# Two experts in four column groups of 32, attention scores over full 128 rows, a subtraction moved to VectorE

## Chip, cores and metric

The kernel runs on one core of a Trainium2 chip, as one launch. The metric is the device time in microseconds (us). Before the change the median of three runs was 2307.31 us (2302.57 to 2308.02). The profile shows one further execution of the same program.

## What is computed

256 tokens of width 1024 in fp32 go through two blocks. The first has a convolution, a forgetting attention and a mixture of 32 experts (four per token); of it the change touches only one place in the code. The second block, cut to what matters:

```python
def second_block(x, ...):
    x = layer_norm_2(x, ln_emb_g, ln_emb_b)
    for layer in range(2):
        mix = hybrid_mixer(x, w_in[layer], ..., decay_fwd[layer], decay_bwd[layer], ...)
        x = layer_norm_2(DEEPNORM_ALPHA * x + mix, ln1_g[layer], ln1_b[layer])
        ffn = swiglu(x, ...) if layer == 0 else moe_swiglu(x, ...)
        x = layer_norm_2(DEEPNORM_ALPHA * x + ffn, ln2_g[layer], ln2_b[layer])

def moe_swiglu(x, router_w, router_b, w1, w3, w2):      # 8 experts, width 1408, two per token
    logits = x @ router_w + router_b
    top_vals, top_idx = lax.top_k(logits, 2)
    gate = ...                                          # softmax of the two, 0 elsewhere
    for e in range(8):
        out = out + gate[..., e:e + 1] * ((silu(x @ w1[e]) * (x @ w3[e])) @ w2[e])
```

The mixer holds a windowed attention (8 query heads, 2 key heads of width 64: scores = q kᵀ / 8) and a retention whose decays are log_sigmoid(decay_fwd) and log_sigmoid(decay_bwd). With the reference's own inputs the router gives the 8 experts of the second block 57, 123, 49, 9, 8, 49, 165 and 52 tokens.

## The kernel before

**Products.** Where full precision is wanted, each fp32 operand is split into a high part that TensorE takes in one pass (type fp32r) and a low rest. A product is then three matmuls, high·high, high·low, low·high (`mm3`, L305 to L307); the weights are split on the fly by a cast on ACT (L325) and a subtraction on DVE (L328). Where few rows stand against many weights, the weights are used unsplit as fp32 moving data (types f32 on both sides), which appear in the trace as two records for each matmul.

**Weights.** `load` (L243) brings tiles of 128 x 2048 fp32 (1 MB) on SP's DMA queue into a ring; in the second mixture the ring has 8 tiles. A tile's load waits on SP until the ring's tile is released, and the loads stand in a fixed order on the queue.

**Order of the work.** The program is written against a Tile layer whose scheduler fixes the order of the instructions on each engine by costs of its own; the code's order is its input. So an edit in one place can reorder work that it doesn't name.

**Stages** (us from the start of the span): preparation, conditioning and the first block's mixer 0 to 250, the first mixture 250 to 1221, mixer 0 of the second block to 1440, its dense part to 1633, mixer 1 to 1837, second mixture's router and expert 0 to 1929, experts 1, 2 and 3 to 2095, experts 4, 5 and 6 to 2252, expert 7 to 2289, the last norm to the end.

**Mixer.** For each pair of heads j the scores are 8 matmuls (L1358 and L1359, taken in turn): `qa[:, j, i]` holds 64 rows of the query's high part and 64 of its low part, `kk[:, i]` the key's high part on both halves, so L1358 takes two of the three products over 128 rows. L1359 takes the third, the query's high part with the key's low part, over 64 rows. `kk` is filled at L1308 (ACT) and L1310 (DVE). There are 8 pairs in the two mixers. The decays' log_sigmoid (L287 to L302, tile `lsg`) stands at the start of the second block, into `lgam`.

**Second mixture.** Experts are sorted by their number of tokens, and `ROOM2` gives the room of each position p: expert 1, the largest, takes all 256 rows (`expert_all`), 0, 4, 5, 6 have room for 128 (`expert_128`), 2, 3 and 7, the smallest, room for 64 (`expert_64`). A token that finds no room goes to an extra loop at the end (L1817), which takes a chunk of up to 128 rows through `expert_128`; the loop's count is read on the chip. Rows are gathered by one-hot matmuls (`gather2`, L1589 to L1605) from `xtp`, the split of the normed input, whose low part is a GpSimd subtraction (L1569).

`expert_64` has weights of two hidden tiles f in hand (each 128 wide, gate and up beside each other: 256 columns). For each of 8 k it issues one matmul per f, with the 64 gathered rows as stationary operand and 256 columns of weights moving (L1732); f even goes to columns 0 to 63 of the array, f odd to 64 to 127. `finish` takes silu on ACT, multiplies on DVE, transposes on PE (L1718), copies on ACT. For the second product (L1748), 512 columns move, the halves of the output in the two column groups. FT2 is 11, so the sixth f-pair has one f. Expert 1's steps alternate with those of 2 and 3: one step of expert 1 (48 mm3 matmuls), then two steps of the others (one f-pair, since an f-pair is two steps).

Of the kernel before, what the change touches and what calls it, by code (L numbers as in the profile page):

```python
# [19 lines left out]
P = 128  # L20
# [19 lines left out]
ROOM2 = [128, 256, 64, 64, 128, 128, 128, 64]  # L40
# [175 lines left out]
def two_blocks(ctx: ExitStack, tc: tile.TileContext, I, out, dbg=None, upto=None):  # L216
# [47 lines left out]
    xres = keep.tile([P, 2, D], F32, name="xres")  # L264
    nc.sync.dma_start(cols, I["cols"])
# [613 lines left out]
    with ExitStack() as pb:  # L879
# [217 lines left out]
        for p in range(NE1):  # L1097
            while (p, CHK1[p][-1]) not in ready or group[2] and p in [g[0] for g in group[1]]:
                gather_on(8)
            if p == 0:  # L1100
                w1, w2 = first_w1, (lambda kk: first_w[8 + kk])
            elif p < FIX1:
                w1 = lambda k: second_w[k] if k < PRE1 else load(I["wei"][p, k * P:(k + 1) * P, :])
                w2 = lambda kk: load(I["weo"][p, kk * 256:(kk + 1) * 256, :].rearrange("(k p) d -> p k d", p=P))
            else:
                er = nc.sync.value_load(route.oi[0:1, p:p + 1], min_val=0, max_val=NE1 - 1)
                w1 = lambda k: load(I["wei"][bass.ds(er, 1), k * P:(k + 1) * P, :].rearrange("a p c -> p (a c)"))
                w2 = lambda kk: load(I["weo"][bass.ds(er, 1), kk * 256:(kk + 1) * 256, :].rearrange("a (k p) d -> p (a k) d", p=P))
            expert1(w1, w2, [ready[p, c] for c in CHK1[p]], lambda: places(p), b1p[:, p] if p else b10, gather_on)
            if p == 8:  # L1110
                second_biases()
                route.extra()
                n_extra = nc.values_load(route.tot[0:1, 0:1], min_val=0, max_val=16, skip_runtime_bounds_check_because="at most 1024 / 64 chunks")
# [43 lines left out]
    with ExitStack() as pc:  # L1157
# [101 lines left out]
        lgam = wc.tile([P, 32], F32, name="lgam")  # L1259
        log_sigmoid(wc, lgam, small[:, SMALL["dec0"][0]:SMALL["dec0"][0] + 32], 32, "sq")  # L1260

        def mixer(l):
            with ExitStack() as pm_:
# [29 lines left out]
                kk = wk.tile([P, 3, S], F32R, tag="kk", name="kk")  # L1293
# [6 lines left out]
                def done(t, a):  # L1300
# [5 lines left out]
                    elif t == 4:  # L1306
                        for i, (r, o) in enumerate(((lo, hi), (hi, lo))):
                            A.mul(kk[r, i], a[r], 0.125)  # L1308
                            A.mul(kk[o, i], a[r], 0.125)
                            V.scalar_tensor_tensor(kk[r, 2], a[r], 0.125, kk[r, i], op0=ALU.mult, op1=ALU.subtract)  # L1310
# [218 lines left out]
        def moe2():  # L1529
            with ExitStack() as pe_:  # L1530
# [45 lines left out]
                def gather2(items, big=None):  # L1576
# [14 lines left out]
                    for (_, room, _), o in zip(items, where):  # L1591
                        xs.append(wk.tile([P, 8, 64], F32, tag="mx64", name=nm("mx64"), bufs=3) if room == 64
                                  else tuple(t[:, :, o:o + 128] for t in big))
                    for k in range(8):
# [5 lines left out]
                        for (_, room, _), o, x in zip(items, where, xs):  # L1600
                            if room == 64:
                                A.copy(x[:, k], pt[:, o:o + 64])
# [5 lines left out]
                def back(item):  # L1608
# [6 lines left out]
                    V.tensor_scalar(gt, pt[:, 0:S], KA["slot"][:, 0:1] if room == 64 else KA["icol"], None, op0=ALU.is_equal)  # L1615
# [136 lines left out]

                def weights(er):
# [14 lines left out]
                def expert(p):  # L1768
# [7 lines left out]
                    return (expert_64 if ROOM2[p] == 64 else expert_128)(w13, w2, ready[p], lambda: item(p))  # L1776
# [24 lines left out]
                while run(every, 1, lambda: gather_group((4, 5))):  # L1801
                    for _ in range(2):
# [5 lines left out]
                run(expert(5), 99, lambda: gather_group((6,)))  # L1808
# [64 lines left out]
```

## Time and profile before

| | |
|---|---|
| median of three runs | 2307.31 us |
| the profiled execution | 2308.48 us |
| its span in the trace | 2306.7 us |
| mean granted TensorE clock | 0.96 |
| PE busy | 2143.9 us, 93% |
| DVE busy | 1125.6 us, 49% |
| ACT busy | 785.1 us, 34% |
| mean DMA rate | 302 GB/s |

Busy time is the union of an engine's records; a matmul's record is longer than its share of a stream, since matmuls overlap, so the time of a stretch is best read from the start of its first record to the start of what follows. The span is 1.8 us shorter than the execution's own time. Lines are those of the kernel before; in the changed kernel the same code stands one to three lines lower up to `expert_64`, and 52 lower behind the new function.

### The profile page before, as it was taken

Reading aid. Unit: us, or ns where it says so; the run is one execution under the profiler, and the core shown is the slowest. Engines: PE = TensorE matmul, PEld = TensorE weight load, DVE = VectorE, ACT = ScalarE, POOL = GpSimd, SP = SyncE. Lnnn points to the kernel's source line nnn. Section 1 sums busy time; section 2 is a strip of 40 time slices with the busy share of each in tenths; the row PEclk is TensorE's granted clock in tenths of the full one; section 3 lists DMA queues with packets and bytes.
Section 4 is the critical chain, followed back from the end, with each engine's and each line's share of the span. In section 5 each row is a group of like instructions: output and inputs, shape, how many; then the busy total and the mean of one; then the engine's idle time right before and its main releaser. Section 6 shows DMA issues by size and latency. Waiting matters only on the chain. (4 is left out here: it accounts for less than half of the span.)

```text
span 2306.7 us, 34090 instructions
## 1 busy us (share of the span) xinstructions
PE 2143.9 (93%) x13530; PEld 1420.7 (62%) x13530; DVE 1125.6 (49%) x2048; ACT 785.1 (34%) x1313; POOL 34.9 (2%) x45
## 2 busy tenths in 40 slices
PE   7999998899999999988887999999999899999996
PEld 5888533233333333333326988998888788778993
DVE  3976223223222332322226657654655775337883
ACT  3345211101111111111104655444465564335771
POOL 0000000000000000000000010000001100000000
PEclk8999999998999999998997999999999989999998
DMA  9756699999999999999997334555533466789884
GB/s 395 287 206 270 238 346 416 416 409 405 416 416 417 416 415 416 416 415 416 416 416 284 136 105 152 201 188 187 185 117 126 155 243 256 283 314 349 324 334 195
DMA packets 122630, 697.52 MB, mean 302 GB/s; under 512 B 11120, under 2 KB 11648, under 8 KB 63936
## 3 DMA queue, kind: packets, MB, share of 16 engines
q1 hardware_dynamic: 121120, 690.54, 76.7%
q0 software_dynamic: 1344, 4.73, 0.6%
q8 instruction: 109, 1.79, 0.3%
q14 instruction: 57, 0.47, 0.1%
HBM read 694.18 MB, written 1.05 MB: 301 GB/s over the span
## 5 line engine op out<-in xcount | busy, mean ns | idle before, releaser
L328 DVE TENSOR_TENSOR wl<-w,wh 128x1024 fp32r<-128x1024 f32 (+1 forms) x393 | 477.0, 1223 | 254.9 <-ACT wh L325 251.7
L325 ACT CAST wh<-w 128x1024 fp32r<-128x1024 f32 (+1 forms) x393 | 407.5, 1045 | 303.9 <-PE acc L306 72.9
L962 PE MATMUL h<-w,xg 128*64 128x512 f32 x1280 | 294.7, 602 | 9.3 <-DMA w<-in_wei 9.3
L997 PE MATMUL s<-w,hm 128*64 128x512 f32 (+1 forms) x1088 | 250.5, 650 | 22.8 <-DVE xres L1030 12.5
L962 PEld LDWEIGHTS h<-w,xg 128*64 128x64 f32 x1280 | 90.6, 138 | 192.1 <-issue 161.2
L973 ACT COPY hs<-h 128x512 f32<-128x512 f32 x34 | 19.9, 585 | 383.2 <-PE h L962 270.4
L305 PE MATMUL acc<-xTh,wh 128*128 128x256 f32 x528 | 149.8, 284 | 0.0
L306 PE MATMUL acc<-xTl,wh 128*128 128x256 f32 x528 | 149.8, 284 | 0.0
L307 PE MATMUL acc<-xTh,wl 128*128 128x256 f32 x528 | 149.8, 284 | 0.0
L997 PEld LDWEIGHTS s<-w,hm 128*64 128x64 f32 (+1 forms) x1088 | 62.0, 132 | 136.3 <-issue 95.6
L973 DVE COPY hs<-h 128x512 f32<-128x512 f32 x20 | 13.8, 691 | 235.2 <-PE h L962 235.2
L956 PE MATMUL h<-w,xg 128*32 128x512 f32 x896 | 114.1, 639 | 9.4 <-DMA w<-in_wei 9.2
L910 PEld LDWEIGHTS t<-oh,xh 128*128 128x128 f32 x512 | 69.3, 205 | 82.5 <-ACT xg L911 33.7
L911 ACT ACTIVATE xg<-t,modc,a 128x128 f32<-128x128 f32 (+3 forms) x128 | 55.0, 440 | 156.4 <-PE t L910 130.4
L1010 DVE TENSOR_TENSOR ys<-s,g2s 128x512 f32<-128x512 f32 x34 | 23.5, 691 | 161.3 <-PE s L997 161.2
L307 PEld LDWEIGHTS acc<-xTh,wl 128*128 128x128 f32 x528 | 99.3, 188 | 4.2 <-issue 3.1
L305 PEld LDWEIGHTS acc<-xTh,wh 128*128 128x128 f32 x528 | 99.3, 188 | 2.5 <-issue 1.5
L306 PEld LDWEIGHTS acc<-xTl,wh 128*128 128x128 f32 x528 | 99.3, 188 | 2.0 <-issue 1.1
L910 PE MATMUL t<-oh,xh 128*128 128x128 f32 (+3 forms) x512 | 85.5, 306 | 14.9 <-ACT xg L911 8.2
L305 PE MATMUL f<-fxh,wh 128*128 128x256 f32 x352 | 98.6, 281 | 0.7 <-ACT fxh L1236 0.7
L307 PE MATMUL f<-fxh,wl 128*128 128x256 f32 x352 | 98.4, 280 | 0.3 <-DVE wl L328 0.3
L306 PE MATMUL f<-fxl,wh 128*128 128x256 f32 x352 | 98.5, 280 | 0.0
(540 smaller groups left out, 4303.6 us busy)
## 6 DMA issues: line engine op xcount, KB each, us to landing
w<-in_wei SPq DMA_DIRECT2D x256, 1024.0 KB, 19.2
w<-in_weo SPq DMA_DIRECT2D x128, 1024.0 KB, 20.0
w<-in_wm SPq DMA_DIRECT2D x128, 1024.0 KB, 6.3
w<-in_wf SPq DMA_DIRECT2D x33, 1024.0 KB, 4.8
w<-in_w2in SPq DMA_DIRECT2D x32, 1024.0 KB, 4.9
w<-in_wada SPq DMA_DIRECT2D x24, 1024.0 KB, 9.2
w<-in_win SPq DMA_DIRECT2D x16, 1024.0 KB, 8.8
w<-in_w2out SPq DMA_DIRECT2D x8, 1024.0 KB, 4.9
```

The source lines that it names most:

```text
L305: T.matmul(o, l[0], r[0], start=start, stop=False)
L306: T.matmul(o, l[0], r[1], start=False, stop=False)
L307: return T.matmul(o, l[1], r[0], start=False, stop=stop)
L325: A.copy(wh[:, :m], w[:, o:o + m])
L328: V.tensor_sub(wl[:, :m], w[:, o:o + m], wh[:, :m])
L910: T.matmul(pt[:, 0:n], xh2[:, tt, k * P:(k + 1) * P], oh[:, tt, 0:n], start=tt == 0, stop=tt == 1)
L911: taken.append(A.activation(xg[:, k, 0:n], pt[:, 0:n], AF.Identity, bias=sh2[:, k:k + 1], scale=a2[:, k:k + 1]))
L956: T.matmul(ph[0][0][32 * q:32 * q + 32, :].rearrange("p (i c) -> p i c", i=4), chunks[0][:, k], w5[:, q % 2, q // 2], start=k == 0, stop=k ...
L962: T.matmul(p[j][64 * gu:64 * gu + 64, :], xs[:, k], w[:, gu * D + j * 512:gu * D + j * 512 + 512], start=k == 0, stop=k == 7)
L973: (A.copy if j == 0 else V.tensor_copy)(hs[:, j], p[j])
L997: T.matmul(p[r, :], hm[:, kk * 2 + k], w[:, k * D + hf * 512:k * D + hf * 512 + 512], start=kk == 0 and (small or k == 0), stop=kk == 3 an ...
L1010: V.tensor_tensor(ys, p, g2s, op=ALU.mult)
```

## The change

Four things are changed.

- **Room.** Positions 2 and 3 get room for 32 instead of 64, in a new `expert_32`: four column groups of 32, gate and up and two f side by side, 128 columns moving in each matmul; for the second product the two halves of the output for even and for odd f, summed at the end. The grouping of the gathers changes (7 goes from the group with 2, 3 to that with 6), and expert 1's steps are taken two at a time, the others' four at a time.
- **Scores.** The key's low part gets two slots, each zero on the other half of the rows, so that L1359's product runs over all 128 rows (L1362 after).
- **Subtraction.** The low part of `xtp` is made by DVE instead of GpSimd.
- **Decays.** log_sigmoid of the second block's decays stands in the code of the first mixture, at p == 8.

```diff
@@ module level
-ROOM2 = [128, 256, 64, 64, 128, 128, 128, 64]
+ROOM2 = [128, 256, 32, 32, 128, 128, 128, 64]
@@ start of the kernel
     xres = keep.tile([P, 2, D], F32, name="xres")
+    lgam = keep.tile([P, 32], F32, name="lgam")
@@ first mixture, after expert p == 8
                 second_biases()
+                log_sigmoid(wk, lgam, small[:, SMALL["dec0"][0]:SMALL["dec0"][0] + 32], 32, "lsg")
@@ second block, before the mixers
-        lgam = wc.tile([P, 32], F32, name="lgam")
-        log_sigmoid(wc, lgam, small[:, SMALL["dec0"][0]:SMALL["dec0"][0] + 32], 32, "sq")
@@ mixer
-                kk = wk.tile([P, 3, S], F32R, tag="kk", name="kk")
+
+                kk = wk.tile([P, 4, S], F32R, tag="kk", name="kk")
+                zk = wk.tile([64, S], F32, tag="zk", name="zk")
+                G.memset(zk, 0.0)
...
                             A.mul(kk[r, i], a[r], 0.125)
                             A.mul(kk[o, i], a[r], 0.125)
-                            V.scalar_tensor_tensor(kk[r, 2], a[r], 0.125, kk[r, i], op0=ALU.mult, op1=ALU.subtract)
+                            V.scalar_tensor_tensor(kk[r, 2 + i], a[r], 0.125, kk[r, i], op0=ALU.mult, op1=ALU.subtract)
+                            A.copy(kk[o, 2 + i], zk)
...
-                            r = slice(64 * i, 64 * i + 64)
                             o = sc[i][:, tt * S:(tt + 1) * S]
                             T.matmul(o, qa[:, j, i, tt * P:(tt + 1) * P], kk[:, i], start=True, stop=False)
-                            T.matmul(o, qa[r, j, i, tt * P:(tt + 1) * P], kk[r, 2], start=False, stop=True)
+                            T.matmul(o, qa[:, j, i, tt * P:(tt + 1) * P], kk[:, 2 + i], start=False, stop=True)
@@ second mixture
                     A.copy(xtp[0][:, tt], xres[:, tt])
-                    G.tensor_tensor(xtp[1][:, tt], xres[:, tt], xtp[0][:, tt], op=ALU.subtract)
+                    V.tensor_sub(xtp[1][:, tt], xres[:, tt], xtp[0][:, tt])
...
+                def expert_32(w13, w2, xg, item):
+                    hm = wk.tile([P, 12, 32], F32, tag="mhm32", name=nm("mhm32"), bufs=2)
+                    def finish(f0, nf, ph):
+                        r = slice(0, 64 * nf)
+                        s = wk.tile([P, P], F32, tag="ms", name=nm("ms"), bufs=2)
+                        A.copy(s[r], ph[r, 0:P])
+                        pt = bank()
+                        T.transpose(pt[:, r], s[r], ident[r, r])
+                        p4 = pt[:, r].rearrange("p (f g s) -> p f g s", g=2, s=32)
+                        s = wk.tile([P, 2, 32], F32, tag="msg", name=nm("msg"), bufs=2)
+                        A.activation(s[:, 0:nf], p4[:, :, 0], AF.Silu)
+                        V.tensor_tensor(hm[:, f0:f0 + nf], s[:, 0:nf], p4[:, :, 1], op=ALU.mult)
...
+                        for k in range(8):
+                            for fi, w in enumerate(ws):
+                                for gu in range(2):
+                                    r, c = 64 * fi + 32 * gu, k * S + gu * P
+                                    T.matmul(ph[r:r + 32, 0:P], xg[:, k], w[:, c:c + P], start=k == 0, stop=k == 7)
...
+                            for hf in range(2):
+                                r, c = 64 * hf + 32 * fi, fi * D + hf * 512
+                                T.matmul(py[r:r + 32, :], hm[:, f], w[:, c:c + 512], start=f0 == 0, stop=f >= FT2 - 2)
...
-                    gather_group((2, 3, 7))
+                    gather_group((2, 3))
...
-                while run(every, 1, lambda: gather_group((4, 5))):
-                    for _ in range(2):
+                while run(every, 2, lambda: gather_group((4, 5))):
+                    for _ in range(4):
                         while few and not run(few[0], 1):
                             few.pop(0)
...
-                run(expert(5), 99, lambda: gather_group((6,)))
+                run(expert(5), 99, lambda: gather_group((6, 7)))
```

**TensorE, experts 1 to 3.** The end of one block of expert 2 before: `w_…` are weight tiles, `mx` the 64 gathered rows, `mxh`/`mxl` the input of expert 1, `ms` what `finish` transposes.

```order
L307 MATMUL b_15216<-mxh_14221,wl_15213 128x256
L1732 MATMUL b_15272<-w_15273,mx_2494_14860 64x256
L1732 MATMUL b_15272<-w_15275,mx_2494_14860 64x256
...
L1718 MATMUL t_15296<-cz,ms_15293 128x128
L305 MATMUL b_15309<-mxh_14221,wh_15301 128x256
L306 MATMUL b_15309<-mxl_14222,wh_15301 128x256
```

And the same place now (`x2` stands for gate and up):

```order
L308 MATMUL b_15191<-mxh_14229,wl_15188 128x256
L1784 MATMUL b_15248<-w_15249,mx_2494_14866 32x128 x2
L1784 MATMUL b_15248<-w_15251,mx_2494_14866 32x128 x2
...
L1784 MATMUL b_15285<-w_15286,mx_2494_14866 32x128 x2
L1784 MATMUL b_15285<-w_15288,mx_2494_14866 32x128 x2
...
L1765 MATMUL t_15324<-cz,ms_15322 128x128
L306 MATMUL b_15339<-mxh_14229,wh_15331 128x256
```

Before, a block of 16 matmuls stands between two groups of 48 mm3 matmuls of expert 1, and the transpose of the block before follows it. Now two blocks of 32 matmuls stand behind each other between groups of 96, and each block multiplies two weight tiles as before.

**VectorE, router of the second mixture, before.** `rowg`, `xres` are the rows being normed, `mxl` the low part of the transposed input that the router multiplies, `wl` the low part of expert 0's first weights.

```order
L1178 SCALAR_TENSOR_TENSOR rowg_14165<-xres,nmn_14187,rowg_14165 128x1024
L328 TENSOR_TENSOR wl_14406<-w_14403,wh_14405 128x1024
L275 TENSOR_SCALAR rstd_14193<-ss_14189 128x1
L1548 TENSOR_TENSOR wr_2371_14214<-wr_14211,wr_2370_14213 128x256
L1182 SCALAR_TENSOR_TENSOR xres<-rowg_14165,pw_14195,rowb_14167 128x512 x2
L1236 TENSOR_TENSOR mxl_14222<-t_14223,mxh_14221 128x4x128
L1236 TENSOR_TENSOR mxl_14222<-t_14230,mxh_14221 128x4x128
L1236 TENSOR_TENSOR mxl_14222<-t_14237,mxh_14221 128x4x128
L1236 TENSOR_TENSOR mxl_14222<-t_14244,mxh_14221 128x4x128
L328 TENSOR_TENSOR wl_14410<-w_14403,wh_14409 128x1024
```

The same stretch now:

```order
L1180 SCALAR_TENSOR_TENSOR rowg_14173<-xres,nmn_14195,rowg_14173 128x1024
L1572 TENSOR_TENSOR xtl_14339<-xres,xth_14338 128x1024
L276 TENSOR_SCALAR rstd_14201<-ss_14197 128x1
L1551 TENSOR_TENSOR wr_2371_14222<-wr_14219,wr_2370_14221 128x256
L1184 SCALAR_TENSOR_TENSOR xres<-rowg_14173,pw_14203,rowb_14175 128x512 x2
L1238 TENSOR_TENSOR mxl_14230<-t_14231,mxh_14229 128x4x128
L1238 TENSOR_TENSOR mxl_14230<-t_14238,mxh_14229 128x4x128
L1572 TENSOR_TENSOR xtl_14339<-xres,xth_14338 128x1024
L329 TENSOR_TENSOR wl_14414<-w_14411,wh_14413 128x1024
L1238 TENSOR_TENSOR mxl_14230<-t_14245,mxh_14229 128x4x128
L1238 TENSOR_TENSOR mxl_14230<-t_14252,mxh_14229 128x4x128
```

The first subtraction takes the place of a weight's low part ahead of `rstd`; the second and a weight's low part now stand between the second and the third `mxl`.

**VectorE, start of mixer 0, before.** `lsg` is the tile of the log_sigmoid, `xTl` the low part of the mixer's transposed input.

```order
L289 TENSOR_SCALAR lsg_7967<-small 128x32
L328 TENSOR_TENSOR wl_8020<-w_7688,wh_8019 128x960
L1182 SCALAR_TENSOR_TENSOR xres<-xres,pw_7962,w_7686 128x512 x2
L290 TENSOR_TENSOR lsg_7967<-lsg_7967,small 128x32
L1236 TENSOR_TENSOR xTl<-t_8005,xTh 128x4x128
L1236 TENSOR_TENSOR xTl<-t_8012,xTh 128x4x128
L328 TENSOR_TENSOR wl_8024<-w_7688,wh_8023 128x960
L292 TENSOR_SCALAR lsg_7967<-lsg_7967 128x32
L301 TENSOR_SCALAR lsg_7967<-small 128x32
```

And now:

```order
L329 TENSOR_TENSOR wl_8020<-w_7715,wh_8019 128x960
L1184 SCALAR_TENSOR_TENSOR xres<-xres,pw_7989,w_7713 128x512 x2
L1238 TENSOR_TENSOR xTl<-t_8005,xTh 128x4x128
L1238 TENSOR_TENSOR xTl<-t_8012,xTh 128x4x128
L329 TENSOR_TENSOR wl_8024<-w_7715,wh_8023 128x960
```

The `lsg` instructions are gone from here. In the changed order they stand among the routing of the first mixture, and the load of ACT's table for exp, which came with them, now stands in mixer 0 ahead of the first softmax (L1374).

## Rows read from the trace of the kernel before

**Rows 1.** The page: busy us, share, instructions; group: count, busy us, mean ns.

```profile
PE 2143.9 (93%) x13530; PEld 1420.7 (62%) x13530; DVE 1125.6 (49%) x2048; ACT 785.1 (34%) x1313; POOL 34.9 (2%) x45
...
L328 DVE TENSOR_TENSOR wl<-w,wh 128x1024 fp32r<-128x1024 f32 (+1 forms) x393 | 477.0, 1223 | 254.9 <-ACT wh L325 251.7
```

**Rows 2.** Stages: length; PE, PEld, DVE, ACT, POOL busy; PEclk, DMA share, GB/s.

```profile
250.00:1221.00 971.00, 880.59 (x4502) 338.12 (x4502) 283.64 (x628) 123.50 (x265) 0.30 (x1) 0.94 1.00 404
1221.00:1440.00 219.00, 205.13 (x1506) 183.01 (x1504) 146.97 (x278) 124.37 (x209) 10.33 (x10) 0.96 0.46 163
...
1633.00:1837.00 204.00, 201.54 (x1496) 180.18 (x1496) 133.04 (x238) 116.93 (x198) 9.50 (x10) 0.99 0.44 153
...
1929.00:2095.00 166.00, 164.40 (x1122) 121.18 (x1119) 63.88 (x110) 51.34 (x107) 0.00 (x0) 1.00 0.78 300
2095.00:2252.00 157.00, 156.36 (x1090) 143.32 (x1090) 140.42 (x161) 113.66 (x145) 0.00 (x0) 1.00 0.91 335
```

**Rows 3.** All waits of PE, 1929 to 2095: total us, times, longest.

```profile
PE b L1662 <- ACT my0h L1656: 1.5, 2, 0.8
```

**Rows 4.** DMA queue, 1929 to 2095: packets, MB, share of 16 engines.

```profile
q1 hardware_dynamic: 8942, 49.54, 77.3%
```

**Rows 5.** Group of line 1732 on PE, 1928.5 to 2094.8: busy us, mean ns, idle.

```profile
L1732 PE MATMUL b<-w,mx 128*64 128x256 f32 x352 | 44.1, 382 | 0.0
```

**Rows 6.** Timeline of PE at first products: start us, us, line, tile.

```profile
1947.66 3.67 PE L1732 MATMUL b<-w,mx 128*64 128x256 f32 x32
1951.26 0.33 PE L1718 MATMUL t<-cz,ms 128*128 128x128 f32 x1
...
2063.82 3.67 PE L1732 MATMUL b<-w,mx 128*64 128x256 f32 x16
```

**Rows 7.** Timeline of PE at a second product.

```profile
1989.57 3.65 PE L1748 MATMUL b<-w,mhm 128*64 128x512 f32 x16
1993.16 0.39 PE L305 MATMUL b<-mxh,wh 128*128 128x256 f32 x1
```

**Rows 8.** Timeline of PE, four groups of 32 in the first mixture.

```profile
339.87 2.35 PE L956 MATMUL h<-w,xg 128*32 128x512 f32 x20
```

**Rows 9.** Timeline of PE, two groups of 64 with 128 columns.

```profile
1387.84 1.97 PE L1447 MATMUL t<-cz,nrst 128*64 128x128 f32 x32
1389.74 0.38 PE L305 MATMUL acc<-ath,wh 128*128 128x256 f32 x1
```

**Rows 10.** Line 646: ns min/median/max, first and last start us.

```profile
L646 PE MATMUL tr<-modc,wr x16: 170/170/191, 191.6 to 192.1; 128*32 128x1 f32 x16
```

**Rows 11.** Timeline of PE at the scores of a pair of heads.

```profile
1291.98 0.28 PE L305 MATMUL acc<-xTh,wh 128*128 128x256 f32 x1
...
1292.33 0.28 PE L1358 MATMUL sc<-kk,qa 128*128 128x256 f32 x1
1292.54 0.38 PE L1359 MATMUL sc<-kk,qa 64*128 64x256 f32 x1
...
1294.73 0.39 PE L305 MATMUL acc<-xTh,wh 128*128 128x256 f32 x1
```

**Rows 12.** Line 1359, and who waited for it (us, times).

```profile
L1359 PE MATMUL sc<-kk,qa x32: 378/380/386, 1292.5 to 1728.4; 64*128 64x256 f32 x32
...
  DVE s L1369: 5.3, 6
```

**Rows 13.** Timelines of DVE and POOL at the second mixture's router.

```profile
1837.19 3.37 DVE L328 TENSOR_TENSOR wl<-w,wh 128x1024 fp32r<-128x1024 f32 x1
1840.48 0.14 DVE L275 TENSOR_SCALAR rstd<-ss 128x1 f32<-128x1 f32 x1
...
1836.84 2.63 POOL L1569 TENSOR_TENSOR xtl<-xres,xth 128x1024 fp32r<-128x1024 f32 x1 [2.72 <-ACT xth L1568]
```

**Rows 14.** Tile lsg, 1232.40 to 1240.40: DVE and ACT busy us.

```profile
1232.40:1240.40 8.00, 1.04 (x6) 0.23 (x1) 0.50 1.02 421
```

**Rows 15.** Line 1308 on ACT: ns min/median/max.

```profile
L1308 ACT ACTIVATE kk<-acc x4: 377/378/378, 1271.2 to 1671.1; 64x256 fp32r<-64x256 f32 x4
```

More of the change, by code (lines that the diff above doesn't have):

```diff
@@ L1591, in gather2 @@
                     for (_, room, _), o in zip(items, where):
-                        xs.append(wk.tile([P, 8, 64], F32, tag="mx64", name=nm("mx64"), bufs=3) if room == 64
+                        xs.append(wk.tile([P, 8, room], F32, tag=f"mx{room}", name=nm(f"mx{room}"), bufs=1 if room == 64 else 2) if room < 128
                                   else tuple(t[:, :, o:o + 128] for t in big))
@@ L1600, in gather2 @@
                         for (_, room, _), o, x in zip(items, where, xs):
-                            if room == 64:
-                                A.copy(x[:, k], pt[:, o:o + 64])
+                            if room < 128:
+                                A.copy(x[:, k], pt[:, o:o + room])
                             else:
@@ L1614, in back @@
                     gt = wk.tile([P, S], F32R, tag="mgt", name=nm("mgt"), bufs=3)
-                    V.tensor_scalar(gt, pt[:, 0:S], KA["slot"][:, 0:1] if room == 64 else KA["icol"], None, op0=ALU.is_equal)
+                    V.tensor_scalar(gt, pt[:, 0:S], KA["icol"] if room == 128 else KA["slot"][:, 0:1] if room == 64 else KA["slot"][:, 2:3], None, op0=ALU.is_equal)
                     return gt, gate
@@ L1751, in expert_64 @@
                     spread([py], *gt, [(0, slice(0, 64)), (0, slice(64, P))])
+                def expert_32(w13, w2, xg, item):
[10 more added lines that the diff above has]
+                        V.tensor_tensor(hm[:, f0:f0 + nf], s[:, 0:nf], p4[:, :, 1], op=ALU.mult)
+                    pend = []
+                    for f0 in range(0, FT2, 2):
+                        nf = min(2, FT2 - f0)
+                        ph = bank("b", 6)
+                        ws = []
+                        for fi in range(nf):
+                            ws.append(load(w13(f0 + fi)))
+                            if fi < nf - 1:
+                                yield "step"
+                        for k in range(8):
[3 more added lines that the diff above has]
+                                    T.matmul(ph[r:r + 32, 0:P], xg[:, k], w[:, c:c + P], start=k == 0, stop=k == 7)
+                        while pend:
+                            finish(*pend.pop(0))
+                        pend = [(f0, nf, ph)]
+                        yield "step"
+                    gt = back(item())
+                    py = bank("b", 6)
+                    for f0 in range(0, FT2, 2):
+                        nf = min(2, FT2 - f0)
+                        w = load(w2(f0, nf), nf * D)
+                        while pend:
+                            finish(*pend.pop(0))
+                        for fi in range(nf):
+                            f = f0 + fi
+                            for hf in range(2):
+                                r, c = 64 * hf + 32 * fi, fi * D + hf * 512
+                                T.matmul(py[r:r + 32, :], hm[:, f], w[:, c:c + 512], start=f0 == 0, stop=f >= FT2 - 2)
+                        yield "step"
+                    spread([py], *gt, [(0, slice(0, 64)), (0, slice(64, P))])
@@ L1775, in expert @@
                         return expert_all(w13, w2, columns(route2.gp, p))
-                    return (expert_64 if ROOM2[p] == 64 else expert_128)(w13, w2, ready[p], lambda: item(p))
+                    return {128: expert_128, 64: expert_64, 32: expert_32}[ROOM2[p]](w13, w2, ready[p], lambda: item(p))
                 def run(gen, steps=99, half=None):
```

## The prediction, made before the changed kernel ran

> **What bounds the kernel now.** I read the page first: PE is busy for 93% of the span [rows 1], so the question is in which stages TensorE itself sets the time. The table of stages answers it [rows 2]. In both mixers of the second block PE is busy for nearly all of the time (205.1 of 219 us, 201.5 of 204 us), in experts 1 to 3 for 164.4 of 166, at full clock. In that last stage the list of PE's waits has one entry, 1.5 us [rows 3]: no weight tile is waited for. The DMA queue of the stage needs 77.3% of 166 us, so 128 us if it never rested [rows 4]. So in these three stages PE's own time counts one to one, and experts 1 to 3 can't fall much under 128 us. Both large edits are edits of PE's time there.
>
> The sum is made against the profiled execution, 2308.5 us, which is 1.2 us above the median of the runs, 2307.3; the span is 1.8 us shorter than the execution.
>
> **Experts 2 and 3, first product.** A block of one f-pair takes 3.60 us, from its first record to the transpose behind it [rows 6]. The block with one f alone has half the records, 16 instead of 32, and the same 3.67 us of busy time [rows 6]: two column groups do run at once, and a record of 256 columns lasts some 0.22 us however many run beside it. All of it is 352 records, which is 11 full blocks of 32; with the single f of each expert there are 12 blocks, 43.2 us by 3.60 (the view by groups says 44.1, [rows 5]). Now a block has 64 records of 128 columns in four groups. If four run at once, the block is 16 quads. A quad is bounded from below by the first mixture's four groups: 20 records of 512 columns in 2.35 us [rows 8], 0.47 per quad with its tail, so about 0.12 for a quarter of the columns, 1.9 us for a block; half of a pair's 0.22 gives 1.8. If records were the limit, the fastest stream in the trace is that of line 646, 16 records within 0.5 us, some 32 ns each [rows 10]: 2.0 us. The slow bound is line 1447, 128 columns in two groups, 32 records in 1.90 us or 59 ns each [rows 9]: 3.8 us, but there half the groups can't show more, a pair takes 0.12 us. I take 1.9 us, the value on which quads and the fast record rate nearly agree: 12 x (3.60 - 1.90) = 20.4 us gained; ends +22 (1.8) and -2.4 (3.8).
>
> **Second product.** 16 records take 3.59 us [rows 7], 0.45 a pair. An expert has 11 f of two halves of two records, so 44 records, 22 pairs, 9.9 us. In four groups ten f make 10 quads and the last f, with only two groups, two pairs: 12 x 0.45 = 5.4 us. Gain 2 x 4.5 = 9.0 us; ends 0 and 10.
>
> **What comes with it.** `finish` has one step more in its chain (copy, transpose, silu, multiply), but two blocks now stand between 96 mm3 matmuls of expert 1, some 11 us in which the chain passes. Where the second block's copy stands behind ACT's casts, PE's transpose may wait 0.2 to 0.4 us per pair of blocks; with six pairs I charge 1.0. The weights: the stage shrinks to 166 - 29 + 1 = 138 us against 128 of DMA, four tiles now go in one burst instead of two, and the ring has eight. I charge 0.5. Gathers: the eight copies of expert 7's rows move from expert 0's half to expert 5's, where ACT has room (113.7 of 157 us, [rows 2]) but DVE little (140.4); PE does the same matmuls either way. At most 8 x 0.38 us, what ACT takes for a copy of 64 x 256 [rows 15]; they have slack between matmuls, I charge 0.2. Region: -20.4 - 9.0 + 1.5 = -28 us.
>
> **Scores.** In a stream of mm3 matmuls of 256 columns one starts every 0.117 us, the first score matmul too (1291.98 to 1292.33, with the three matmuls of one product between, [rows 11]). Then it slows: line 1359 starts 0.21 after line 1358, and the eight together take 2.40 us, from 1292.33 to 1294.73 [rows 11]. The only thing that alternates there and not in a stream is 128 against 64 rows. With 128 rows throughout, eight at 0.117 take 0.94: 1.46 us less per pair of heads. The 32 records of line 1359 [rows 12] are eight pairs of heads: 11.7 us. Does the end behind it move too? DVE's softmax waits for these scores six times, 5.3 us in all [rows 12], and not PE for DVE, and between the pairs PE has mm3 streams of the projections. I take 11.5; ends 0 and 12. The zeroed slots cost two ACT copies of 64 x 256 per layer (0.38 us each, [rows 15]) and a GpSimd fill: four copies, 1.5 us of ACT in stages where it is busy 57% of the time; I charge 0.3, ends 0 and 1.5.
>
> **Subtraction.** At the router DVE's subtraction of a weight's low part takes 3.37 us beside GpSimd's 2.63, where its mean is 1.22, and the norm's `rstd` comes only behind it [rows 1, 13]. Everything of the stage waits on `rstd`, the second half of the rows, the transposes, the router. Now the GpSimd one is gone and DVE's own, 1.22 us by the same shape, takes the place: `rstd` is 2.0 us earlier. But the second one and a weight's low part stand ahead of the last two `mxl`, where DVE waited on ACT before: about 1 us comes back. Net -1; ends -2 and +1.
>
> **Decays.** In the first 8 us of mixer 0 the log_sigmoid holds DVE for 1.04 us, ACT for 0.23 [rows 14], on a path of norm, transpose, split that DVE sets. Half of it counts, -0.5; ends -1.2 and +0.5, since the table load for exp now comes in front of the first softmax. In the first mixture its place is among routing while DVE is idle; I charge nothing: that stage has its DMA at a share of 1.00 and DVE busy 284 of 971 us [rows 2]. If that cover fails, 1 us.
>
> Sum: -28 (experts) - 11.5 (scores) - 1 - 0.5 + 0.3 + 0.2 (gather) = -40.5. So 2308.5 - 40.5 = 2268.0 in a run like the profiled one, 2267 beside the median.
>
> **Rivals.**
> A: the forecast, chance 0.64; own range 2259 to 2276 (all good ends, 22 + 10 + 12 + 2 + 1 = 47 less; a few of the charges doubled and a quarter of the scores lost, 32 less).
> B: the weights become late in experts 1 to 3. For it: 138 us of PE against 128 of DMA at full share, and bursts of four tiles; the next stage already runs its DMA at a share of 0.91 [rows 2]. Against it: the queue now rests for 23% of the stage [rows 4], and PE waits for no tile. If the lead is used up halfway, the stage falls only to about 150: 12 of 28 us come back, 2279. Chance 0.15.
> C: records are the limit of the four groups. For it, the two-group stream at 59 ns [rows 9]; against it, line 646 at 32 ns [rows 10]. 64 x 59 ns = 3.8 us: the first product gives -2.4 instead of +20.4, 2290. Chance 0.08.
> The Trainium skill, "TensorE: Matmul & The Clock Gate", section "Wait — 56ns, not 53.3ns?", names a floor of about 25 ns from one matmul's start to the next, and about 62 ns where the sequencer decodes matmuls in microcode. By the second rule a block would take 64 x 62 ns = 4.0 us and C would hold; the 32 ns of line 646 speak for the first.
> D: the scores' gain is given back. PE reaches the softmax earlier and waits there for DVE and ACT, with the table load ahead of the first exp; 5 of 11.5 us stay, 2274. For it: DVE and ACT are busy 67% and 57% of mixer 0 [rows 2]; against it: DVE waits for PE, not PE for DVE [rows 12]. Chance 0.08.
> E, the slower side: one of the two experts has more than 32 tokens. Then the rest takes a chunk of the extra loop, with all its weights and 128 rows at the end of the kernel, where nothing runs beside it. Three experts of that room take 157 us in the trace [rows 2], so one takes 52, with gather and loop some 57: 2267 + 57 = 2324. It decides at 33 tokens; the two experts have 9 and 8 with the reference's inputs. Chance 0.02. The remaining 0.03 is a stall of the kind that I can't name, anywhere between 2276 and 2310.
>
> **How the numbers follow.** The forecast is A's 2267. The range 2257 to 2284 holds nearly all of A and D and most of B, 0.62 + 0.08 + 0.11, about 0.8; C, E and the unnamed stay outside. A difference of 0.3%, 7 us, is about what a measurement of this kernel can tell from no change. A, B and D are faster by 29 us or more, C by 18; together 0.95, less a little for B and C at their worst: faster 0.94, same 0.03, slower 0.03 (E and half of the unnamed).
>
> **What would show it.** PE's timeline: a block of 64 records of the new w13 line in 1.8 to 2.0 us, the second product in about 0.9 us per f-pair; a block at 3.8 is C. Stage from expert 1 to the end of expert 3: 138 us, with no PE waits on weight tiles; waits named after `in_wm` of several us are B. Scores: eight matmuls at 0.94 us instead of 2.40, and both mixers 5.8 us shorter; if the mixers shrink by less, D. Router: DVE's weight subtraction back at 1.22 us. A last loop that runs, with its gather and 50 us of matmuls, is E. The prediction is wrong if the four groups take more than 2.4 us a block or the stage is above 145 us.

## The result and the profile after

The changed kernel took 2272.43 us in the median of four runs (2270.3 to 2276.11), the kernel before 2307.66 us in four; the ratio is 0.9857, 95% interval 0.9845 to 0.987. Measured again later, beside other kernels, the ratio was 0.9835 (0.9819 to 0.9851). The forecast was 2267 us with a range of 2257 to 2284.

The profiled execution took 2276.11 us, the slowest of the four, with a span of 2274.2; before it was 2308.48 and 2306.7. To see where the 32.5 us went, the table cuts both spans at the same places: the first matmul of each stage that begins with a transposition of the normed rows, and the first matmul of the output of each expert, `spread` (L1662 before, L1665 after). Each number is a difference of two starts in PE's timeline, in us.

| stretch | before | after | difference |
|---|---|---|---|
| up to mixer 0 (first mixture in it) | 1230.58 | 1232.15 | +1.57 |
| mixer 0 | 207.22 | 200.12 | -7.10 |
| dense part | 192.91 | 193.75 | +0.84 |
| mixer 1 | 204.98 | 198.65 | -6.33 |
| router, expert 0 | 84.73 | 83.79 | -0.94 |
| to the output of expert 2 | 90.01 | 81.05 | -8.96 |
| to the output of expert 3 | 82.95 | 62.30 | -20.65 |
| to the output of expert 4 | 50.28 | 55.66 | +5.38 |
| to the output of expert 5 | 55.33 | 57.51 | +2.18 |
| to the output of expert 6 | 50.92 | 50.93 | +0.01 |
| to the output of expert 7 | 38.30 | 39.81 | +1.51 |

The start of mixer 0 lies anywhere from 1223.1 to 1232.2 us in the executions profiled here, with the same code before it or nearly so: the first mixture varies by that much. The experts' stages repeat to some tenths of a us where the order of the instructions is the same, the mixers to about 1, and the dense part took 192.9 to 194.9 us, with one execution at 197.1. So the parts of the change are better read from stages than from whole times.

Stages of the changed kernel, to be held against [rows 2] (length; PE, PEld, DVE, ACT, POOL busy; PEclk, DMA share, GB/s):

```profile
1223.00:1433.00 210.00, 197.63 (x1503) 180.35 (x1504) 140.78 (x253) 123.47 (x207) 10.53 (x11) 0.96 0.47 170
...
1908.00:2053.00 145.00, 142.47 (x1529) 119.18 (x1528) 64.44 (x115) 49.31 (x109) 0.00 (x0) 1.00 0.86 336
2053.00:2216.00 163.00, 157.76 (x1088) 144.39 (x1084) 142.56 (x163) 114.84 (x156) 0.00 (x0) 0.98 0.91 341
```

Experts 1 to 3 are short and PE is still busy in them. (This row starts at the output of expert 0, 8.6 us earlier in the work than the row from 1929 in [rows 2]; cut at like places, the stage went from 174.3 to 144.8 us.) Experts 4 to 6, of which the diff touches nothing but one gather, grew from 157 to 163 us, with PE idle for 5 of them and a mean granted clock (PEclk) of 0.98 instead of 1.00.

The new first product on PE, against [rows 6], and a second product, against [rows 7]:

```profile
1937.75 1.96 PE L1784 MATMUL b<-w,mx 128*32 128x128 f32 x64
1939.63 0.33 PE L1765 MATMUL t<-cz,ms 128*128 128x128 f32 x1
...
1955.56 1.94 PE L1784 MATMUL b<-w,mx 128*32 128x128 f32 x32
1957.43 0.33 PE L1765 MATMUL t<-cz,ms 128*128 128x128 f32 x1
...
1972.16 3.64 PE L1801 MATMUL b<-w,mhm 128*32 128x512 f32 x32
1975.73 0.39 PE L306 MATMUL b<-mxh,wh 128*128 128x256 f32 x1
```

A block of 64 records takes 1.88 us from its start to the transpose, 29 ns for a record; with one f, 32 records in two groups, it takes 1.87. The starts in the trace show why: in the full block records start in fours, some 7 ns apart, in the block with one f in twos, and the next four, or two, starts 0.109 us after the one before. 32 records of the second product take 3.57 us, where 16 took 3.59. Both are the forecast's values (1.9 us, and 0.45 us for four records).

The scores, against [rows 11]:

```profile
1293.30 0.28 PE L1361 MATMUL sc<-kk,qa 128*128 128x256 f32 x1
1293.42 0.28 PE L1362 MATMUL sc<-kk,qa 128*128 128x256 f32 x1
...
1294.13 0.28 PE L1362 MATMUL sc<-kk,qa 128*128 128x256 f32 x1
1294.25 0.28 PE L306 MATMUL acc<-xTh,wh 128*128 128x256 f32 x1
```

Eight matmuls take 0.95 us instead of 2.40, one every 0.119 us, like the products around them.

What was not forecast is in the waits of PE from the end of expert 3 on (total us, times, longest). Before, this list has three entries, 2.0 us in all, and none on a weight. The largest after:

```profile
PE b L307 <- DVE wl L329: 3.8, 2, 3.4
PE t L1721 <- DVE ms L1719: 1.4, 2, 0.7
PE b L306 <- ACT wh L326: 1.0, 1, 1.0
PE b L1665 <- ACT my0h L1659: 1.0, 2, 0.7
```

The 3.4 us stand at the start of expert 4. The timelines of ACT, DVE and PE there:

```profile
2042.84 1.04 ACT L326 CAST wh<-w 128x1024 fp32r<-128x1024 f32 x1
2051.17 0.59 ACT L1659 CAST my0h<-b 128x512 fp32r<-128x512 f32 x1 [7.29 <-PE b L1801]
2051.65 3.88 ACT L326 CAST wh<-w 128x1024 fp32r<-128x1024 f32 x4
...
2053.07 2.73 DVE L1668 SCALAR_TENSOR_TENSOR xres<-b,gp,xres 128x512 f32<-128x512 f32 x4 [0.59 <-PE b L1665]
2055.71 4.62 DVE L329 TENSOR_TENSOR wl<-w,wh 128x1024 fp32r<-128x1024 f32 x4
...
2053.20 0.38 PE L306 MATMUL b<-wh,mxh 128*128 128x256 f32 x1
2056.98 0.58 PE L307 MATMUL b<-wl,mxh 128*128 128x256 f32 x1 [3.40 <-DVE wl L329]
```

ACT's next instruction is the cast of expert 3's output (`my0h`), and it waits 7.3 us for PE. The casts of expert 4's weights stand behind it and run at 2051.65. DVE then does four accumulations of expert 3 before the first low part of expert 4's weights.

The wait costs more than its 3.4 us. While PE stood idle the granted clock fell to 0.50, the lower of its two levels (1.2 instead of 2.4 GHz), and stayed there until 2061. At that level one matmul starts every 0.21 us, behind it one every 0.12 (the row of PEclk first, then PE):

```profile
2055.00:2061.00 6.00, 4.02 (x19) 4.02 (x20) 5.52 (x7) 1.58 (x2) 0.00 (x0) 0.50 1.01 425
...
2060.35 0.41 PE L307 MATMUL b<-wl,mxh 128*128 128x256 f32 x1
2060.56 0.41 PE L308 MATMUL b<-wh,mxl 128*128 128x256 f32 x1
...
2061.28 0.27 PE L306 MATMUL b<-wh,mxh 128*128 128x256 f32 x1
2061.39 0.28 PE L307 MATMUL b<-wl,mxh 128*128 128x256 f32 x1
```

The 19 steps from 2056.98 to 2060.99 take 4.01 us, where 19 at 0.119 take 2.26. So of the 5.4 us lost at expert 4, 3.4 are the wait and about 1.7 the clock behind it. All executions here with this order show such a stretch of half clock at expert 4's start; the kernel before, and the four versions below in which two casts of expert 4 stand ahead of expert 3's output, show none there.

In the kernel before, the order of ACT was the other way round: four casts of expert 4 stood ahead of expert 3's output (three of them shown).

```profile
2076.52 1.04 ACT L325 CAST wh<-w 128x1024 fp32r<-128x1024 f32 x1 [2.28 <-DMA w<-in_wm]
...
2083.41 1.04 ACT L325 CAST wh<-w 128x1024 fp32r<-128x1024 f32 x1 [1.75 <-PE b L307]
2089.99 1.04 ACT L325 CAST wh<-w 128x1024 fp32r<-128x1024 f32 x1 [5.54 <-PE b L307]
2092.73 0.58 ACT L1656 CAST my0h<-b 128x512 fp32r<-128x512 f32 x1 [1.69 <-PE b L1748]
```

At expert 5 the same difference is smaller: three casts of its weights stood ahead of expert 4's output before, one does now. In expert 7, PE now issues the first matmul of a block, then the transpose of the block before it, which waits for DVE, and then the rest (start, us, and the wait in brackets):

```profile
2225.76 0.65 PE L1735 MATMUL b<-w,mx 128*64 128x256 f32 x2
2226.33 0.33 PE L1721 MATMUL t<-cz,ms 128*128 128x128 f32 x1
2226.59 3.67 PE L1735 MATMUL b<-w,mx 128*64 128x256 f32 x32
2230.95 0.33 PE L1721 MATMUL t<-cz,ms 128*128 128x128 f32 x1 [0.68 <-DVE ms L1719]
```

Before, a transpose followed the whole next block, and waited for nothing. The records x32 here are 30 of one block and 2 of the next.

### The profile page after: what moved, and what is told of

Same layout as the page of the kernel before. It is cut to its first block, busy times and chain, and to the rows that moved or that the text cites. A ratio compares the mean times of both kernels' runs of the same rounds, so it can differ in the third digit from the quotient of the medians.

```text
span 2274.2 us, 34778 instructions
## 1 busy us (share of the span) xinstructions
PE 2105.5 (93%) x13882; PEld 1411.1 (62%) x13882; DVE 1122.5 (49%) x2050; ACT 782.0 (34%) x1317; POOL 30.4 (1%) x45
## 5 line engine op out<-in xcount | busy, mean ns | idle before, releaser
L329 DVE TENSOR_TENSOR wl<-w,wh 128x1024 fp32r<-128x1024 f32 (+1 forms) x393 | 472.2, 1217 | 187.3 <-ACT wh L326 184.4
L998 PE MATMUL s<-w,hm 128*64 128x512 f32 (+1 forms) x1088 | 257.0, 665 | 23.5 <-DVE xres L1031 12.8
L974 ACT COPY hs<-h 128x512 f32<-128x512 f32 x34 | 19.9, 586 | 377.5 <-PE h L963 275.2
L957 PE MATMUL h<-w,xg 128*32 128x512 f32 x896 | 107.8, 613 | 5.0 <-DMA w<-in_wei 5.0
## 6 DMA issues: line engine op xcount, KB each, us to landing
w<-in_weo SPq DMA_DIRECT2D x128, 1024.0 KB, 19.9
```

The costliest lines, as they stand in the source:

```text
L329: V.tensor_sub(wl[:, :m], w[:, o:o + m], wh[:, :m])
L957: T.matmul(ph[0][0][32 * q:32 * q + 32, :].rearrange("p (i c) -> p i c", i=4), chunks[0][:, k], w5[:, q % 2, q // 2], start=k == 0, stop=k ...
L974: (A.copy if j == 0 else V.tensor_copy)(hs[:, j], p[j])
L998: T.matmul(p[r, :], hm[:, kk * 2 + k], w[:, k * D + hf * 512:k * D + hf * 512 + 512], start=kk == 0 and (small or k == 0), stop=kk == 3 an ...
```

## Experiments

A seam is the place where one expert ends and the next begins. Theory O: the 9.1 us lost in experts 4, 5 and 7 come from the order that the scheduler gave to instructions which the diff doesn't name. Theory W, the forecast's rival B: they come from weights that land late. All ratios are to the kernel before, run beside them.

**Scores alone** (the kernel before with the mixer's hunks of the diff).

> The kernel before with the scores over 128 rows alone. Forecast's step: eight score matmuls in 0.94 us instead of 2.40 for each of eight pairs of heads, so 11.7 us less, about 2296 us. Rival (given back in the softmax): at most 5 us less, about 2302 us, with PE waits on DVE or ACT in the mixers that were not there before.

Measured: 2294.01 us beside 2304.38, ratio 0.9956 (0.9942 to 0.997). Mixer 0 took 200.82 us, mixer 1 198.83, the dense part 193.36: together 12.1 less than before, and the experts were unchanged (367.72 us from the output of expert 0 to that of 7, 367.79 before). The forecast's 11.7 stands; the softmax gave nothing back.

**Room alone** (the kernel before with `ROOM2`, `expert_32`, the interleave and the gathers of the diff).

> The kernel before with only the room of 32 (expert_32, interleave of two and four steps, groups of the gather). In the changed kernel experts 1 to 3 gained 29.6 us and experts 4, 5 and 7 lost 5.4, 2.2 and 1.5. If these losses belong to this part, the net is 20.5 less, about 2287 us, with the same order of ACT's casts behind expert 3's output. If they need the other parts, about 2278 us.

Measured: 2285.62 us, ratio 0.9923 (0.9907 to 0.9939). Outputs of expert 0 to 7: 81.18, 62.30, 56.13, 57.52, 50.93 and 39.80 us, the changed kernel's stages to half a us. Gains and losses both belong to this part. Mixer 0 and 1 were 0.6 and 1.0 us shorter than before with nothing changed in them, which is the spread of these stages. By whole times, scores and room give 10.4 and 18.8 us, 29.2 of the 35.2 that the whole change gave; by stages it is 12.1 and 19.9 of 34.1, and the subtraction and the decays bring most of the rest. Why the whole times leave more open isn't shown; the spread of the first mixture is large enough for it.

**First casts pinned.** `issue_after` puts an instruction behind another on its engine:

```diff
+                                order.enter_context(tc.issue_after(ins.ins))   # for ins in pins
                             A.copy(ys[i][0], pyb)
...
-                while few:
-                    run(few.pop(0))
-                run(expert(4))
+                run(few[0], 2)
+                fourth = expert(4)
+                run(fourth, 1)
+                pins[:] = casts[-2:]
+                while few:
+                    run(few.pop(0))
+                pins.clear()
+                run(fourth)
```

> The changed kernel, with the two casts of expert 4's first weight tile put ahead of the cast of expert 3's output on ACT; the loads are the same. Theory O (order): the 5.4 us lost at the start of expert 4 come from these casts standing behind an instruction that waits 7.3 us for TensorE; expert 4 takes 51 us again instead of 56.2 and the whole is 5 us less than the changed kernel, about 2267 us; expert 5 and 7 stay as they are. Theory W (weights): the ring's lead is used up and the tiles land late; TensorE then waits for the tile instead, expert 4 stays at 56 us, the whole at 2272.

Measured: 2266.11 us, ratio 0.983 (0.9816 to 0.9843). The outputs of experts 3 and 4 come after 65.28 and 47.71 us, 112.99 together against 117.96 in the changed kernel: 5.0 us back. (Expert 3's output now falls into expert 4's first matmuls, so only the sum compares.) Expert 5 and 7 stay at 57.54 and 39.81. ACT's timeline there:

```profile
2039.53 1.04 ACT L326 CAST wh<-w 128x1024 fp32r<-128x1024 f32 x1
2043.28 2.00 ACT L326 CAST wh<-w 128x1024 fp32r<-128x1024 f32 x2 [2.71 <-DMA w<-in_wm]
2047.86 0.58 ACT L1662 CAST my0h<-b 128x512 fp32r<-128x512 f32 x1 [2.58 <-PE b L1804]
```

ACT waits for the tile's DMA, until 4.5 us before expert 4's first matmul (2047.74); in the kernel before, the same cast ran at 2076.52, 18.2 us ahead of that matmul (2094.75). So W has a part of the truth, the lead of the loads has shrunk; but the tile is still there and cast before the output can be. What cost the 5 us was O: without the wait, the stretch of half clock is gone too.

**Six steps for two** (experts 2 and 3 end before expert 1):

```diff
-                    for _ in range(4):
+                    for _ in range(6):
```

> The changed kernel with six steps instead of four of experts 2 and 3 for two steps of expert 1, so that these two end before expert 1 does. Theory O: the cast of expert 3's output no longer stands in front of expert 4's casts, and in expert 7 the transposes stand in front of the next block again as before the change: expert 4 at 51 us, expert 7 at 35.8, about 7 us less than the changed kernel, 2265 us, if weights are no limit. Theory W: three blocks for 96 mm3 matmuls need 8 tiles in 18 us, 466 GB/s, above the 417 GB/s of the busiest stretches; TensorE waits for tiles in the first product's rounds, 2 us in each of four, up to 8 us, which cancels the gain: 2271 to 2275 us.

Measured: 2273.5 us, ratio 0.9859 (0.9841 to 0.9877): no gain, and a time within W's range. Outputs: 57.10, 70.09, 76.16, 55.74, 50.93, 38.88. Expert 5 and 7 got most of their time back, but the wait moved to the place where the output of expert 2 now stands ahead of casts for expert 1's weights. PE's waits from 1885 to 2110, where most of expert 1 to 4 lies:

```profile
PE b L308 <- DVE wl L329: 4.0, 2, 3.3
PE b L306 <- ACT wh L326: 1.2, 1, 1.2
PE b L1665 <- ACT my0h L1659: 1.1, 3, 0.7
```

No entry names a tile's DMA, so W's cause isn't seen though its time is. The wait of 3.3 us is again followed by half clock. The prediction of O for this kernel was wrong in its sum: an end that is taken away from one seam is put at another.

**Two groups at a time** (the same 64 records of a block, gate of both f first, then up):

```diff
-                        for k in range(8):
-                            for fi, w in enumerate(ws):
-                                for gu in range(2):
+                        for gu in range(2):
+                            for k in range(8):
+                                for fi, w in enumerate(ws):
```

> The changed kernel with the same 64 records per block in another order: gate of both f for all eight k, then up, so that neighbours fill two column groups and not four. If the gain comes from four groups at once, a record takes 56 to 59 ns as in line 1447, a block 3.6 to 3.8 us, and experts 1 to 3 are 21 us longer (12 x 1.8). If the records run together whatever their order, the block stays at 1.88 us.

Measured (one execution): 2280.87 us. The block:

```profile
1931.02 3.29 PE L1784 MATMUL b<-w,mx 128*32 128x128 f32 x64
1934.24 0.33 PE L1765 MATMUL t<-cz,ms 128*128 128x128 f32 x1
```

3.22 us instead of 1.88, 50 ns for a record; the outputs of experts 2 and 3 come after 88.40 and 68.98 us, 14.0 us later than with four neighbours. The size was overestimated (3.6 to 3.8 us), and the starts in the trace show by what: pairs follow each other every 0.109 us, but in the middle of the block, where the last pairs of gate run beside the first of up, four steps hold four records, so the block has 28 steps and not 32. The cause stands: four groups at once, and not fewer bytes or columns, are the gain.

**Subtraction back on GpSimd** (`G.tensor_tensor` in place of `V.tensor_sub` for `xtp`).

> The changed kernel with the subtraction back on GpSimd. Forecast: router and expert 0 are 1 us longer (2 us on rstd, 1 us given back at the last mxl); the bounds were 2 us and -1. DVE's subtraction of a weight's low part beside it takes 3.4 us again instead of 1.2. The 0.9 us by which this stage shrank in the changed kernel could also be noise of the stage: then it stays at 83.8.

Measured (one execution): router and expert 0 85.24 us against 83.79 and 83.57 in two executions of the changed kernel: 1.5 to 1.7 us, inside the bounds. Not all of that is shown to be the subtraction's. The stage has two stretches at a granted clock of 0.50, and the second lasts 10.2 us here and 6.8 in those two executions. Where the gathers and this stretch are alike, GpSimd's subtraction costs 0.6 to 0.9 us (84.39 in the kernel with room alone, against 83.47 to 83.79), 1.1 (85.24 against 84.18) and 0.2 to 0.4 (84.73 and 84.92 against 84.56). What is sure is the forecast's first step: `rstd` starts 4.80 us after the stage's start here and 2.65 in the changed kernel, 2.15 earlier. DVE's timeline at the router of this kernel, and of the changed one behind it:

```profile
1825.28 3.37 DVE L329 TENSOR_TENSOR wl<-w,wh 128x1024 fp32r<-128x1024 f32 x1
1828.57 0.14 DVE L276 TENSOR_SCALAR rstd<-ss 128x1 f32<-128x1 f32 x1
```

```profile
1826.18 1.22 DVE L1572 TENSOR_TENSOR xtl<-xres,xth 128x1024 fp32r<-128x1024 f32 x1
1827.32 0.15 DVE L276 TENSOR_SCALAR rstd<-ss 128x1 f32<-128x1 f32 x1
...
1831.93 1.22 DVE L329 TENSOR_TENSOR wl<-w,wh 128x1024 fp32r<-128x1024 f32 x1
```

**Decays back in mixer 0** (`log_sigmoid` at its old place).

> The changed kernel with the log_sigmoid of the second block's decays back at the start of mixer 0. Forecast: mixer 0 gained 0.5 us by its move (bounds -1.2 and +0.5), so mixer 0's stage is 0.5 us longer than in the changed kernel (200.1 to 200.6 us there), and the first mixture, bound by its DMA, is the same within its spread of some us. If the work had only been moved in front of another wait, mixer 0 stays the same.

Measured (one execution): 2269.67 us, mixer 0 200.88 us against 200.12 and 200.55: 0.3 to 0.8 us, as forecast. All ten executions here with the new scores and the decays moved took 199.89 to 200.63 us, 200.29 in the mean; this one and that of the scores alone, both with the decays in mixer 0, took 200.88 and 200.82.

**Steps as before** (`run(every, 1, ...)` and `range(2)`).

> The changed kernel with the steps as before the change: one of expert 1, two of the others. Blocks then stand singly between 48 mm3 matmuls. Theory O: here the order puts both casts of expert 4's first tile ahead of the cast of expert 3's output, so expert 4 takes 48 to 51 us instead of 55.7; experts 1 to 3 pay some 0.1 to 0.3 us for each of six more changes between mm3 and blocks, 1 to 2 us. Together about 3 us less than the changed kernel in experts 1 to 4. Theory W: smaller bursts change nothing in the bytes, expert 4 stays at 55.7.

Measured (one execution): 2264.76 us. Outputs of experts 2, 3 and 4 after 74.73, 68.75 and 50.26 us, 193.74 together against 199.01: the 5.4 us at expert 4 are gone, and single blocks cost nothing that shows (143.48 us for the first two, 143.35 with pairs). Expert 5 stays at 57.51, expert 7 at 39.80, with the changed kernel's order there. The coarser interleave of the change gave nothing and cost the stall.

**Gather as before** ((2, 3, 7), (4, 5), (6,)).

> The changed kernel with expert 7's rows gathered with those of 2 and 3 again, instead of with 6. Forecast: worth 0.2 us, so no stage moves by more than 0.5 us; the order of casts and transposes around experts 4, 5 and 7 is that of the changed kernel, so their losses stay. Rival: the gather in expert 5's half is what made expert 5 lose 2.2 us; then its stage falls to 55.3.

Measured (one execution): 2269.31 us; expert 5 56.95, expert 7 39.81, expert 4 55.99. Router and expert 0, which hold that gather again, took 84.56 us against 83.79 and 83.57, so a stage moved by more than the 0.5 us of the forecast; the second stretch of half clock is the longer one here too. The gather's place makes at most 0.6 of the 2.2 us that expert 5 lost.

**All seams in order.** For experts 3, 4 and 5 the next expert's first two casts stand ahead of the output, and in `expert_64` the transposes behind the next block:

```diff
+                        with tc.issue_after(last[0].ins):
                             T.transpose(pt[:, r], s[r], ident[r, r])
...
+                def follow(gen, left, p, half=None):
+                    run(gen, left, half)
+                    nxt = expert(p)
+                    run(nxt, 1)
+                    pins[:] = casts[-2:]
+                    run(gen)
+                    pins.clear()
+                    return nxt
```

> The changed kernel with three places put in order: before the cast of the output of expert 3, 4 and 5 on ACT stand the two casts of the next expert's first weight tile, and in expert 7 each transpose stands behind the next block again. Theory O: expert 4's stage 47 to 48 us as with the first pin alone, expert 5's back from 57.5 to 55.3, the last stage from 39.8 to 38.3; about 3.7 us less than that pin alone, 8.5 less than the changed kernel, ratio to the kernel before about 0.982. Theory W (late tiles): expert 5 and 7 stay at 57.5 and 39.8, ratio 0.9835 as with the first pin.

> The changed kernel once more, beside its reordered version on the same chip: ratio 0.9857 to the kernel before, experts 4, 5 and the last stage at 55.7, 57.5 and 39.8 us in the trace, since the order is the same; the first mixture may differ by some us.

Measured beside each other on one chip: 2259.66 us, ratio 0.9798 (0.9779 to 0.9817), against 2271.32 us and 0.9835 (0.9819 to 0.9851) for the changed kernel, whose stages repeated (55.34, 57.51, 50.90, 39.81). From the output of expert 0 to that of 7 it takes 337.66 us; the changed kernel 347.26 and 346.92, the kernel before 367.79. So 9.3 to 9.6 us came back, what experts 4, 5 and 7 had lost (9.1) and up to half a us more. The outputs of expert 3 to 7 come after 65.25, 50.45, 54.99, 47.62 and 38.30 us. The last is expert 7's old value; the others have to be summed, since a pinned output falls into the next expert's first matmuls: from expert 2's output to expert 6's it is 218.3 us, 226.4 in the changed kernel and 221.5 with the first pin alone.

**The same with the steps as before the change.**

> The reordered kernel (first casts of the next expert ahead of the output of experts 3, 4 and 5, transposes of expert 7 behind the next block), with the steps as before the change, one of expert 1 and two of the others. Theory O: the grouping of the steps costs or gives nothing by itself, only the order at the seams counts; experts 1 to 4 take 194 us in both, the whole is within 1 us of the reordered kernel with steps of two and four, ratio 0.979 to 0.981. If the smaller bursts of loads are worth something in their own right, it is 2 us or more faster.

Measured: 2261.61 us, ratio 0.9797 (0.9784 to 0.9811); experts 337.01 us, without a stretch of half clock among them. From expert 0's output to expert 4's it takes 196.3 us, 196.8 with steps of two and four: alike, though not the 194 expected. With the seams in order the interleave makes no difference.

## Why the prediction was right, and which step was not

- **First and second product.** Right in mechanism and size: 1.88 us a block, where 1.9 was taken. Experts 1 to 3, from the output of expert 0 to expert 4's first matmul, went from 174.33 to 144.75 us, 29.6 less; the forecast had 28. In the prediction's own cut the stage went to 166 - 29.6 = 136.4, where 138 was forecast and 145 was the sign of being wrong. Rival C, a bound on records of 59 ns [rows 9], is out: 29 ns. The sum made there with the second rule of the Trainium skill ("TensorE: Matmul & The Clock Gate", "Wait — 56ns, not 53.3ns?") counts records for matmuls: a block's 64 records are 32 matmuls. By that rule, some 62 ns for a matmul, the estimate is 2.0 us and not 4.0, and C would not have held. The trace doesn't decide between the two rules: the block's 1.88 us are 59 ns for a matmul, near 62, while its records start 7 ns apart within a four, below the 25 of the first.
- **What comes with it.** This step failed. It charged 1.5 us for stalls and lateness inside experts 1 to 3, 0.5 of it for the weights, and nothing behind them. Experts 4, 5 and 7 lost 9.1 us, some 1.7 of them to half clock behind the wait at expert 4. Rival B came nearest in size (12 us back, in experts 1 to 3) and had the wrong cause: the loads' lead had shrunk, but PE waited for splits, and these for their place in ACT's and DVE's order. The order of the changed kernel shows these seams as well as experts 1 to 3, but the sum was made from experts 1 to 3 alone. The pin shows the cause for expert 4 (5.0 us back), the transposes put back show it for expert 7 (1.5), and the pins of the outputs of experts 4 and 5 bring the rest (3.2 us, where 2.2 had been lost).
- **Scores.** Right: 12.1 us in stages, where 11.7 had been worked out and 11.5 taken. Rival D is out.
- **Subtraction.** Right in kind: `rstd` comes 2.15 us earlier (2.0 forecast), and between before and after the stage shrank by 0.9 (1 forecast), with a shorter stretch of half clock in it. The size isn't settled: 0.2 to 1.1 us where these stretches are alike.
- **Decays.** About 0.6 us by the mean of ten executions, forecast 0.5.
- **Rival E** didn't occur: expert 7's output is followed by the last norm, with no chunk between.
- The sum: forecast -40.5, stages -34.1 from mixer 0 on (13.4 in the mixers, +0.8 dense, 0.9, 20.5 in the experts), and the first mixture 1.6 longer in that execution. That the median came within 5.4 us of the forecast is in part luck: the 9.1 us that were not charged met 1.6 more gained in experts 1 to 3 and about 1 more in the mixers.

Open: why the scheduler turned the order round at the seams. That its costs see the loads late when experts 2 and 3 take less time fits the shrunken lead, but no run here shows its costs.

## What to carry to other kernels

Small stationary operands in four column groups pay when the four are neighbours in TensorE's order; ordering the same records by twos gave back 1.34 of the 1.72 us that a block had gained. When a stage gets shorter under a scheduler, compare the order of every engine at the seams behind it as well, and look for an instruction that waits for the old stage's end ahead of the work that the next stage needs first. A 35 us gain can hide a 9 us loss, which a table by stage shows and the whole time doesn't. And price a wait of TensorE with what follows it: here 3.4 us of waiting cost 5.1, as the clock had fallen.

## What was not expected of the hardware

After a wait of 3.4 us TensorE ran at a granted clock of 0.50 for 4 us of work, with a matmul every 0.21 us instead of 0.12. One stage, router and expert 0, took 0.4 to 0.9 us more where a stretch of half clock in it lasted 10.2 instead of 6.8 us, with the same code in it. The time up to the start of mixer 0, most of it a stage whose DMA is never idle, differed by up to 9 us between executions of nearly the same code (1223.1 to 1232.2), more than most single parts of this change.
